# A hybrid encoder block on one core: the end rewritten, weight splits ordered behind bank readers, two kinds of operands loaded earlier, spilled tiles fetched among the kept

## The chip, the cores and the metric

The kernel runs on one core of a Trainium2 chip. The time is device microseconds of one execution; three runs of the kernel before gave a median of 917.51 us (916.77 to 918.26). The profile is of a further execution, which took 916.25 us. TensorE does the matrix products, VectorE and ScalarE the work on elements, GpSimd (POOL) and SyncE (SP) here mostly issue DMA transfers. Every engine runs its instructions in a fixed order.

## The reference

Two request groups ("prompt" and "sample", 1024 positions by 1024 channels each) go through one layer with shared weights:

```
h = rmsnorm(x, g_pre);  z = h @ w_in                      # 1024 -> 6 x 512
ya = pool_mixer(a_val) * silu(a_gate)                     # window means of 2/4/8/16, 128x128 maps
yb = short_conv(b_u, b_B, b_C) * silu(b_gate)             # width 3
o = concat(ya, yb) @ w_out;  x = x + rmsnorm(o, g_post)
gate = sigmoid(x @ w_ple_gate);  e = (p @ w_ple) * gate
y = x + rmsnorm(e, g_ple)
```

All is fp32. rmsnorm multiplies by 1/sqrt(mean(v*v) + 1e-6) over the 1024 channels and by a gain for each channel.

## The kernel before, in words

Activations lie with channels on the 128 partitions and positions along the free axis; a tile is 128 channels by 1024 positions, or a half of it, 512. An fp32 product is made of three matmuls on rounded parts: each operand is split into a high and a low part (`split`: a cast on ScalarE, L153, and a subtraction on VectorE, L154), and `mm` issues high*high, high*low and low*high at L293 to L295. Weights come from DRAM as raw blocks (`wraw`, three buffers), are split into halves (`whl`, eight buffers) and kept five halves ahead of TensorE (`AHEAD`). A scheduler orders the instructions of most of the program by their priorities; DMA issues and some additions are pinned to program order, and at the start and in the end the order on TensorE, ScalarE and VectorE is written out.

The work comes in stages. Stage A is the input projection of group 0, then of group 1: twelve pairs of weight blocks each. Stage B is the output projection, four pairs each. But for the first pair, a pair is done with seven products in place of eight (`pair_seven`, on sums and differences of operands; weights are summed at L210). A product has 12 matmuls of 128x512. Its seven kinds of operands (`KINDS`: n11, n21, z, t1, t3, t4, n22) are written to DRAM ahead of time, and when a group or a stage ends, 28 of them (4 of each kind) are loaded (`load_unit`) through six small buffers (`s`) and split. `take_place` does that for one kind, as soon as the last pair has used the old one; before the first of them `drain` empties the queue of background steps. A product goes to a bank of PSUM; ScalarE copies three of the results out (L507, L515, L522), and the next product into the same bank waits for that copy, as the bank `y` is used for four products.

The post-norm of group 0 (`norm_b`) runs as background steps inside stage B of group 1: sums of squares are added over the channels by matmuls with a matrix of ones, the root is made with logarithm, exponential and one Newton step (`rstd_l`), and for each of eight tiles VectorE multiplies by gain and root (L728) and GpSimd adds the product to the residual x1 in DRAM (L127). Three of the eight tiles are spilled to DRAM (`od`, `SPILL`), fetched again after the five kept ones are done (L124).

Last comes the gate: pieces of 24 matmuls, for each a sigmoid on ScalarE (L828), a multiply by the other factor (`pled`, loaded from DRAM by SP) on VectorE (L829), a square (L354) and an addition to the sum of squares (L355). The last four pieces of the last half of group 1 are done in two parts of 256 positions each (`finish`), so that the norm and the results of the first part lie beside the matmuls of the second. The results are y = e * r (L935), plus x1 (L937), and stores.

Of the kernel before, what the change touches and what calls it, by code (L numbers as in the profile page):

```python
# [16 lines left out]
P = 128  # L17
# [26 lines left out]

AHEAD = 5
# [4 lines left out]
TAIL = 4  # L50
FILL = 2, 2, 3
# [3 lines left out]
def tile_hybrid_encoder(ctx: ExitStack, tc, x, p, par, w_in, w_pool, w_out, w_gate, w_ple, y):  # L55
# [38 lines left out]
    nc.vector.memset(eps, EPS)  # L94
    one = const.tile([P, P], F32, name="one")
    nc.vector.memset(one, 1.0)
    nc.vector.tensor_copy(out=ones, in_=one)
    nc.scalar.mul(gneg, par_sb[:, G_PRE : G_PRE + KD], -1.0)
# [38 lines left out]

    def col(i):
        return par_sb[:, i : i + 1]
# [11 lines left out]

    def split(hi, lo, src):
        nc.scalar.copy(out=hi, in_=src)  # L153
        nc.vector.tensor_tensor(out=lo, in0=src, in1=hi.bitcast(F32), op=ALU.subtract)  # L154
# [24 lines left out]
    def hl_tile():  # L179
        return wpool.tile([P, 2, H, P], F32R, name="whl", tag="whl", bufs=HLBUFS)  # L180

    def split_half(src):
        hl = hl_tile()
        split(hl[:, 0], hl[:, 1], src)
        return hl
# [114 lines left out]
    def rstd_steps(acc, tmp, out=None, wait=1):  # L300

        n = acc.shape[1]
        u = unit()
        split(u[:, 0, :n], u[:, 1, :n], acc)
        for _ in range(wait):
            yield
        ps = psn.tile([P, C], F32, name="psn")[:, :n]  # L310
        nc.tensor.matmul(ps, ones, u[:, 0, :n], start=True, stop=False)
        nc.tensor.matmul(ps, ones, u[:, 1, :n], start=False, stop=True)
        r, v = (t[:, :n] for t in pair())
        a = tmp
        tc.keep_in_program_order(nc.scalar.preload_act_table_set("natural_log_exp_and_others"))
        nc.scalar.activation(out=r, in_=ps, func=AF.Ln, bias=eps, scale=1.0 / D)
        nc.scalar.activation(out=v, in_=ps, func=AF.Identity, bias=eps, scale=1.0 / D)
        nc.scalar.activation(out=r, in_=r, func=AF.Exp, scale=-0.5)
        yield
        nc.vector.tensor_tensor(out=a, in0=r, in1=v, op=ALU.mult)  # L320
        nc.vector.scalar_tensor_tensor(out=a, in0=a, scalar=-0.5, in1=r, op0=ALU.mult, op1=ALU.mult)
        out = r if out is None else out
        nc.vector.scalar_tensor_tensor(out=out, in0=a, scalar=1.5, in1=r, op0=ALU.add, op1=ALU.mult)
        yield
        return out

    def rstd_l(acc, out, wait=1):
# [6 lines left out]
        v, a = T()[:, :L], T()[:, :L]  # L334
        ps = [psn.tile([P, C], F32, name="psn") for c in range(NCH)]
        for p, u in zip(ps, us):
            nc.tensor.matmul(p, ones, u[:, 0], start=True, stop=False)
            nc.tensor.matmul(p, ones, u[:, 1], start=False, stop=True)
        tc.keep_in_program_order(nc.scalar.preload_act_table_set("natural_log_exp_and_others"))
# [5 lines left out]
        nc.vector.tensor_tensor(out=a, in0=out, in1=v, op=ALU.mult)  # L345
        nc.vector.scalar_tensor_tensor(out=a, in0=a, scalar=-0.5, in1=out, op0=ALU.mult, op1=ALU.mult)
        nc.vector.scalar_tensor_tensor(out=out, in0=a, scalar=1.5, in1=out, op0=ALU.add, op1=ALU.mult)
# [129 lines left out]
    def product(ps, units, first):  # L477
        mm(ps, [next_half()], operand(units), range(H), first, True, not first)
        product_done()

    def emit(dst, ps, add=None, neg=False):

        if add is None:
            nc.scalar.mul(dst, ps, -1.0 if neg else 1.0)
        elif neg:
            nc.vector.scalar_tensor_tensor(out=dst, in0=ps, scalar=-1.0, in1=add, op0=ALU.mult, op1=ALU.subtract)  # L486
        else:
            nc.vector.tensor_tensor(out=dst, in0=ps, in1=add, op=ALU.add)
# [13 lines left out]
    def pair_seven(h, use):  # L502
# [4 lines left out]
        nc.scalar.copy(out=p, in_=y)  # L507
# [7 lines left out]
        nc.scalar.copy(out=u, in_=y)  # L515
# [6 lines left out]
        nc.scalar.copy(out=g, in_=y)  # L522
# [195 lines left out]
    def norm_b(s, acc, kept):  # L718
# [7 lines left out]
        def add(k):  # L726
            pinned(
                nc.vector.scalar_tensor_tensor(  # L728
                    out=got[k], in0=got[k], scalar=col(G_POST + k), in1=r, op0=ALU.mult, op1=ALU.mult
# [26 lines left out]


# [41 lines left out]
    class Gate:  # L799
# [19 lines left out]
        def piece(self, d, c, w, i=0, n=C):  # L819

            o = i * n
            if i == 0 and d % 2 == 0:
                self.fetch()
            e = self.e(c, d)[:, o : o + n]
            z = bank()[:, :n]
            mm(z, w, operand(x1u[self.s][c], o, n), range(KD))
# [22 lines left out]
        def norm(self, c):  # L849

            s = self.s
            r = yield from rstd_steps(self.accs[c], small(), None, 4)
# [9 lines left out]
            for j in range(KD // 2):  # L862
                for i in range(2):
                    e = self.e(c, 2 * j + i)
                    nc.vector.scalar_tensor_tensor(
                        out=e, in0=e, scalar=col(G_PLE + 2 * j + i), in1=r, op0=ALU.mult, op1=ALU.mult
# [7 lines left out]
        def finish(self):  # L874
# [4 lines left out]
            s, c, n = self.s, NCH - 1, C // 2  # L879
# [105 lines left out]
    def run(steps):  # L985
        for _ in steps:
            pass
# [283 lines left out]
```

## Time and profile before

| | |
|---|---|
| median of three runs | 917.51 us |
| profiled execution | 916.25 us, of which 914.4 us is the span from first to last instruction |
| TensorE busy | 876.5 us (96%), 3830 matmuls |
| VectorE busy | 721.9 us (79%) |
| ScalarE busy | 483.5 us (53%) |
| GpSimd busy | 124.4 us (14%) |
| mean granted TensorE clock | 0.990 of 2.4 GHz |

Busy time is the time in which an engine executes something; with TensorE at 96%, what matters is where its few idle microseconds lie, and what it waited for there. Matmuls overlap: a 128x512 matmul is shown with 0.39 us, but the next starts 0.23 us after it. "<-" names what ended a wait: "<-ACT s L522" means that ScalarE's instruction of line 522, writing a tile named s, let it go. PE is TensorE, ACT ScalarE, DVE VectorE, POOL GpSimd, SPq the DMA issues of SP.

### The profile page before, as it was taken

To read this page: it belongs to the slowest core of one execution; us is meant where nothing else is said; L and a number is where in the kernel's file an instruction comes from. 1 tells how busy PE (TensorE), PEld (TensorE's weight loads), DVE (VectorE), ACT (ScalarE), POOL (GpSimd) and SP (SyncE) were. 2 spreads that over 40 slices of the span, in tenths; PEclk is the share of its full clock that TensorE was granted. 3 is DMA by queue.
4 is the path that set the end of the run, shared out by engine and by line. 5 is a ranking of instruction groups with operands and counts; after the bars stand their busy time and mean duration, and the time that the engine had idled before them with its cause. 6 is when DMAs were issued, how large, how long until landed. Compare 5 with 4: busy or idle time off the path is not lost.

```text
span 914.4 us, 11123 instructions
## 1 busy us (share of the span) xinstructions
PE 876.5 (96%) x3830; PEld 706.3 (77%) x3830; DVE 721.9 (79%) x1090; ACT 483.5 (53%) x829; POOL 124.4 (14%) x222
## 2 busy tenths in 40 slices
PE   6999999999999999999999999999998999999992
PEld 4787887888888788888888877887776788888892
DVE  5799999988668998586776988868878675678566
ACT  6967754333335743333333377447735653666743
POOL 0111111330000023201011100100021012013230
PEclk9999999999999999999999999999999999999996
DMA  9751645662215776756244367437398649859994
GB/s 341 294 184 58 200 147 206 217 251 73 89 51 158 253 256 219 265 183 237 97 173 162 128 221 254 180 116 230 115 230 218 220 103 273 268 128 280 295 307 165
DMA packets 65721, 179.31 MB, mean 196 GB/s; under 512 B 7296, under 2 KB 10880, under 8 KB 65664
## 3 DMA queue, kind: packets, MB, share of 16 engines
q1 hardware_dynamic: 39504, 98.84, 31.9%
q0 software_dynamic: 26016, 79.70, 28.9%
q8 instruction: 30, 0.49, 0.2%
q14 instruction: 27, 0.22, 0.1%
q10 hardware_dynamic: 144, 0.05, 0.0%
HBM read 127.72 MB, written 65.54 MB: 211 GB/s over the span
## 4 chain that ended last, share of the span: by engine, by line
PE 80%; DMA 7%; DVE 6%; ACT 4%; issue 2%; SPq 0%; DVEq 0%; ACTq 0%
PE z L293 26%; PE z L295 26%; PE z L294 26%; DMA s<-ykept_t 2%; DMA t<-x_d 1%; ACT u L153 1%; DMA t<-od 1%; DVE u L154 1%; DMA s<-yd 1%; DMA t<-p_d 1%; DVE u L463 1%; DVE t L937 1%; DVE t L728 1%; DMA x1d<-t 1%; DMA s<-kept_z 0%
## 5 line engine op out<-in xcount | busy, mean ns | idle before, releaser
L293 PE MATMUL z<-u,whl 128*128 128x512 f32 (+1 forms) x1188 | 461.6, 390 | 11.4 <-ACT s L522 8.8
L295 PE MATMUL z<-u,whl 128*128 128x512 f32 (+1 forms) x1188 | 460.0, 389 | 0.5 <-DVE whl L154 0.5
L294 PE MATMUL z<-u,whl 128*128 128x512 f32 (+1 forms) x1188 | 460.2, 388 | 0.0
L293 PEld LDWEIGHTS z<-u,whl 128*128 128x128 f32 x1188 | 223.3, 188 | 67.0 <-ACT s L522 12.5
L295 PEld LDWEIGHTS z<-u,whl 128*128 128x128 f32 x1188 | 223.6, 188 | 50.6 <-DVE whl L154 0.9
L294 PEld LDWEIGHTS z<-u,whl 128*128 128x128 f32 x1188 | 223.4, 188 | 49.4
L153 ACT CAST whl<-wsum 128x512 fp32r<-128x512 f32 x124 | 75.7, 619 | 101.3 <-PE z L295 48.4
L153 ACT CAST whl<-wraw 128x512 fp32r<-128x512 f32 x145 | 88.4, 619 | 61.2 <-PE z L295 52.7
L154 DVE TENSOR_TENSOR whl<-wraw,whl 128x512 fp32r<-128x512 f32 x145 | 97.8, 685 | 18.3 <-ACT whl L153 18.1
L154 DVE TENSOR_TENSOR whl<-wsum,whl 128x512 fp32r<-128x512 f32 x124 | 84.0, 685 | 24.6 <-ACT whl L153 24.1
L154 DVE TENSOR_TENSOR u<-s,u 128x512 fp32r<-128x512 f32 x92 | 61.2, 688 | 23.7 <-ACT u L153 22.9
L153 ACT CAST u<-s 128x512 fp32r<-128x512 f32 x92 | 55.3, 619 | 28.0 <-DMA s<-x1d 14.8
L210 DVE TENSOR_TENSOR wsum<-wraw 128x512 f32<-128x512 f32 x62 | 42.6, 687 | 31.0 <-DMA wraw<-w_in_d 26.3
L127 POOL DMA_DIRECT2D x1d<-t x40 | 38.5, 1198 | 204.2 <-DVE t L728 135.4
L153 ACT CAST u<-t 128x512 fp32r<-128x512 f32 x71 | 41.3, 622 | 26.4 <-DVE t L570 9.3
L354 ACT ACTIVATE s<-t 128x512 f32<-128x512 f32 (+1 forms) x60 | 36.1, 603 | 32.4 <-DVE t L829 17.3
L154 DVE TENSOR_TENSOR u<-t,u 128x512 fp32r<-128x512 f32 x71 | 45.6, 685 | 8.8 <-ACT u L153 8.5
L355 DVE TENSOR_TENSOR t<-t,s 128x512 f32<-128x512 f32 (+1 forms) x60 | 39.0, 652 | 10.6 <-ACT s L354 9.5
L124 POOL DMA_DIRECT2D yd<-t x16 | 8.7, 546 | 251.7 <-DVE t L623 166.3
L515 ACT COPY s<-z 128x512 f32<-128x512 f32 x31 | 18.1, 584 | 37.7 <-PE z L295 33.4
L522 ACT COPY s<-z 128x512 f32<-128x512 f32 x31 | 18.1, 583 | 35.9 <-PE z L295 35.9
L486 DVE SCALAR_TENSOR_TENSOR t<-z,s 128x512 f32<-128x512 f32 x46 | 31.4, 684 | 5.7 <-PE z L295 5.7
(121 smaller groups left out, 798.5 us busy)
## 6 DMA issues: line engine op xcount, KB each, us to landing
wraw<-w_in_d SPq DMA_DIRECT2D x48, 512.0 KB, 3.8
wraw<-w_gate_d SPq DMA_DIRECT2D x24, 512.0 KB, 6.1
pled<-t POOLq DMA_DIRECT2D x16, 512.0 KB, 3.8
t<-x_d POOLq DMA_DIRECT2D x16, 512.0 KB, 5.4
yd<-t POOLq DMA_DIRECT2D x16, 512.0 KB, 3.3
t<-yd POOLq DMA_DIRECT2D x16, 512.0 KB, 5.7
x1d<-x_d POOLq DMA_DIRECT2D x8, 1024.0 KB, 11.8
wraw<-w_out_d SPq DMA_DIRECT2D x16, 512.0 KB, 3.7
```

What stands on the lines that cost most here:

```text
L127: pinned(nc.gpsimd.dma_start(out=out, in_=in_, accum_op=ALU.add))
L153: nc.scalar.copy(out=hi, in_=src)
L154: nc.vector.tensor_tensor(out=lo, in0=src, in1=hi.bitcast(F32), op=ALU.subtract)
L210: nc.vector.tensor_tensor(out=t, in0=a, in1=b, op=ALU.add)
L293: nc.tensor.matmul(ps, wk[:, 0, kw, :], hi, start=a, stop=False, skip_group_check=on)
L294: nc.tensor.matmul(ps, wk[:, 0, kw, :], lo, start=False, stop=False, skip_group_check=on)
L295: nc.tensor.matmul(ps, wk[:, 1, kw, :], hi, start=False, stop=z, skip_group_check=on)
L354: nc.scalar.activation(out=tmp, in_=src, func=AF.Square)
L355: nc.vector.tensor_tensor(out=acc, in0=acc, in1=tmp, op=ALU.add)
L486: nc.vector.scalar_tensor_tensor(out=dst, in0=ps, scalar=-1.0, in1=add, op0=ALU.mult, op1=ALU.subtract)
L515: nc.scalar.copy(out=u, in_=y)
L522: nc.scalar.copy(out=g, in_=y)
```

## The change

It has five parts. The names are those of the code; line numbers of the changed kernel are higher by 5 to some 50.

1. *The end* (`finish`). Five pieces in place of four are cut into two parts of 256 positions (`TAIL`, `PARTS`, `FILL`). The sum of squares of a part is taken in two steps into the same place in PSUM: that of the first seven pieces (`most`), and that of the last piece, whose square goes straight into the split (`square`). The root of the first part (`root`) stands amid the matmuls of the second part's first piece. The Newton step reads PSUM. Weights of the two halves beyond eight go into ordinary tiles (`spare`).
2. *Roots.* `rstd_steps` and `rstd_l` no longer make the mean with a pass of ScalarE (Identity); the Newton step reads the sum in PSUM, with the gains multiplied by sqrt(D) once at the start. It is done in halves of 512.
3. *Reader order.* The copies and sums that read a product's bank are noted (`reader`), and a weight split gets an order behind those of the product four back on its own engine, without a semaphore (`behind_readers`).
4. *Early operands.* At a change of group or stage, `after` calls `take_place` two product steps earlier (`EARLY`), so for two kinds in the pair before last, and `drain` with it.
5. *Spilled tiles.* `norm_b` fetches the three spilled tiles after the third, fourth and fifth kept tile's addition, no longer after all five.

```diff
-TAIL = 4
-FILL = 2, 2, 3
+EARLY = 2
+READERS = 5
+TAIL = 5
+PARTS = 256, 256
+FILL = 5, 2, 1, 1, 2
...
+    readers = deque([[]], maxlen=READERS)
...
+    def behind_readers(ins):
+        if len(readers) == READERS:
+            for q in readers[0]:
+                if q.ins.engine == ins.ins.engine:
+                    tc.add_manual_dep(
+                        ins.ins,
+                        q.ins.name,
+                        mybir.DependencyInfo(mybir.DependencyClass.NoSync, mybir.DependencyReason.DATA),
+                        reason="behind a product's readers",
+                    )
...
     def split_half(src):
-        hl = hl_tile()
-        split(hl[:, 0], hl[:, 1], src)
+        if spare:
+            spare.pop()
+            hl = tpool.tile([P, 2, H, P], F32R, name="u", tag="t")
+        else:
+            hl = wpool.tile([P, 2, H, P], F32R, name="whl", tag="whl", bufs=HLBUFS)
+        for ins in split(hl[:, 0], hl[:, 1], src):
+            behind_readers(ins)
         return hl
...
+    def guess(r, ps):
+        nc.scalar.activation(out=r, in_=ps, func=AF.Ln, bias=eps)
+        nc.scalar.activation(out=r, in_=r, func=AF.Exp, scale=-0.5)
+
+    def newton(r, ps, a):
+        nc.vector.scalar_tensor_tensor(out=a, in0=ps, scalar=D * EPS, in1=r, op0=ALU.add, op1=ALU.mult)
+        yield
+        nc.vector.scalar_tensor_tensor(out=a, in0=a, scalar=-0.5, in1=r, op0=ALU.mult, op1=ALU.mult)
+        yield
+        nc.vector.scalar_tensor_tensor(out=r, in0=a, scalar=1.5, in1=r, op0=ALU.add, op1=ALU.mult)
+        yield
...
-        for p, o, w in zip(ps, halves(out), halves(v)):
-            nc.scalar.activation(out=o, in_=p, func=AF.Ln, bias=eps, scale=1.0 / D)
-            nc.scalar.activation(out=w, in_=p, func=AF.Identity, bias=eps, scale=1.0 / D)
-        nc.scalar.activation(out=out, in_=out, func=AF.Exp, scale=-0.5)
+        for p, q in zip(ps, halves(r)):
+            guess(q, p)
+        yield
+        for p, q, a in zip(ps, halves(r), pair()):
+            run(newton(q, p, a))
...
-        for k in range(SPILL[s], KD):
+        spilt = deque(range(0 if s else SPILL[s]))
+        for i, k in enumerate(range(SPILL[s], KD)):
             add(k)
             yield
-            yield
-        for k in range(SPILL[s]):
-            if not s:
-                fetch(k)
-                yield
+            if spilt and i >= 2:
+                fetch(spilt.popleft())
+            yield
...
+                def most(part):
+                    hi, lo = part.us[0]
+                    nc.scalar.copy(out=hi, in_=part.acc)
+                    nc.vector.tensor_tensor(out=lo, in0=part.acc, in1=hi.bitcast(F32), op=ALU.subtract)
+
+                def square(part):
+                    e, (hi, lo) = self.e(c, KD - 1)[:, part.cs], part.us[1]
+                    nc.scalar.activation(out=hi, in_=e, func=AF.Square)
+                    nc.vector.tensor_tensor(out=part.q, in0=e, in1=e, op=ALU.mult)
+                    nc.vector.tensor_tensor(out=lo, in0=part.q, in1=hi.bitcast(F32), op=ALU.subtract)
...
+                for n in PARTS:
+                    part = Part(o, n)
+                    for i, (d, w) in enumerate(zip(last, ws)):
+                        amid = (lambda: root(before)) if before and not i else None
+                        piece = self.piece(d, c, w, o, n, amid)
+                        if d < KD - 1:
+                            run(piece)
+                        else:
+                            next(piece)
+                            total(part.ps, part.us[0], True, False)
+                        if before and not i:
+                            for q in last:
+                                scale(q, before.cs)
+                            steps = before.rest()
+                        if before and d < KD - 1:
+                            fill(FILL[i])
+                        if d == KD - 2:
+                            part.most()
+                    part.square()
+                    before, o = part, o + n
+                root(part)
...
     def after(stage, s, j, n):
         pump(AHEAD)
-        if j == (NPAIR if stage == "A" else KD // 2) - 1:
-            if n == 0:
-                drain()
-                product_done(LATER)
-            take_place(stage, s, n)
-        else:
+        early = 0 if stage == "B" and s else EARLY
+        to_last = (NPAIR if stage == "A" else KD // 2) - 1 - j
+        kind = n + early - to_last * len(KINDS)
+        if kind == 0:
+            drain()
+            product_done(LATER)
+        if 0 <= kind < len(KINDS):
+            take_place(stage, s, kind)
+        if kind < 0:
             tick(1)
```

Three places show how the order of instructions moves. First GpSimd in the post-norm of group 0; `x1d0_...` is the residual that the tiles are added to, `od0_0`, `od0_1` and `od0_2` the spilled tiles. Before:

```order
L127 DMA x1d0_2_122<-t_5118 256x1x512
L127 DMA x1d0_2_122<-t_5175 256x1x512
L127 DMA x1d0_3_123<-t_5262 256x1x512
L127 DMA x1d0_3_123<-t_5399 256x1x512
L124 DMA t_5852<-od0_0_117 128x1024
L124 DMA t_5877<-od0_1_118 128x1024
L124 DMA t_5879<-od0_2_119 128x1024
L127 DMA x1d0_0_120<-t_5852 256x1x512
L127 DMA x1d0_0_120<-t_5877 256x1x512
```

The changed kernel:

```order
L135 DMA x1d0_2_124<-t_5117 256x1x512
L135 DMA x1d0_2_124<-t_5174 256x1x512
L132 DMA t_5727<-od0_0_119 128x1024
L135 DMA x1d0_3_125<-t_5301 256x1x512
L132 DMA t_5764<-od0_1_120 128x1024
L135 DMA x1d0_3_125<-t_5438 256x1x512
L132 DMA t_5837<-od0_2_121 128x1024
L135 DMA x1d0_0_122<-t_5727 256x1x512
L135 DMA x1d0_0_122<-t_5764 256x1x512
```

The fetches have moved from behind the fifth addition to behind the third, fourth and fifth, so the fourth and fifth additions now stand behind fetches.

Second, ScalarE at the change from group 0 to group 1 in stage A; a cast `u<-s` splits a loaded operand, and the copy `s<-z` (L522, L568 after) empties the bank. Before:

```order
L153 CAST u_2608<-s_2607 128x512
L153 CAST whl_2794<-wraw_2548 128x512
L153 CAST u_2613<-s_2612 128x512
L153 CAST u_2618<-s_2617 128x512
L153 CAST u_2623<-s_2622 128x512
L153 CAST whl_2835<-wraw_2502 128x512
L153 CAST u_2655<-s_2654 128x512
L522 COPY s_2686<-z_2467 128x512
L153 CAST u_2660<-s_2659 128x512
```

The changed kernel:

```order
L185 CAST u_2647<-s_2646 128x512
L185 CAST u_2652<-s_2651 128x512
L185 CAST whl_2813<-wraw_2587 128x512
L185 CAST u_2657<-s_2656 128x512
L185 CAST u_2662<-s_2661 128x512
L185 CAST u_2694<-s_2693 128x512
L185 CAST u_2699<-s_2698 128x512
L568 COPY s_2725<-z_2466 128x512
L185 CAST u_2704<-s_2703 128x512
```

Before, the copy stands behind the first cast of the kind t1 (u_2655); after, two kinds more have been loaded, and it stands behind the second cast of t4 (u_2694, u_2699).

Third, VectorE in the end, first part: L829 (L880 after) multiplies a piece by its pled tile (t_7472 before, t_7440 after is the last pled tile loaded). Before:

```order
L829 TENSOR_TENSOR t_7380<-t_7380,s_7517 128x256
L355 TENSOR_TENSOR t_6907<-t_6907,s_7517 128x256
L829 TENSOR_TENSOR t_7380<-t_7380,s_7547 128x256
L355 TENSOR_TENSOR t_6907<-t_6907,s_7547 128x256
L829 TENSOR_TENSOR t_7472<-t_7472,s_7577 128x256
L355 TENSOR_TENSOR t_6907<-t_6907,s_7577 128x256
L829 TENSOR_TENSOR t_7472<-t_7472,s_7607 128x256
L355 TENSOR_TENSOR t_6907<-t_6907,s_7607 128x256
L908 CAST u_7480<-t_6907 128x256
L909 TENSOR_TENSOR u_7480<-t_6907,u_7480 128x256
```

The changed kernel:

```order
L880 TENSOR_TENSOR t_7280<-t_7280,s_7480 128x256
L396 TENSOR_TENSOR t_6907<-t_6907,s_7480 128x256
L880 TENSOR_TENSOR t_7378<-t_7378,s_7510 128x256
L396 TENSOR_TENSOR t_6907<-t_6907,s_7510 128x256
L880 TENSOR_TENSOR t_7378<-t_7378,s_7540 128x256
L396 TENSOR_TENSOR t_6907<-t_6907,s_7540 128x256
L880 TENSOR_TENSOR t_7440<-t_7440,s_7570 128x256
L396 TENSOR_TENSOR t_6907<-t_6907,s_7570 128x256
L963 TENSOR_TENSOR u_7453<-t_6907,u_7453 128x256
L880 TENSOR_TENSOR t_7440<-t_7440,s_7602 128x256
L969 TENSOR_TENSOR t_7452<-t_7440 128x256
```

Before, the first multiply with the last pled tile (d=6) belongs to the third half piece, and a whole piece (d=3) stands ahead of the three; now it belongs to the fourth half piece, and d=3 is a half as well. The subtraction for the ones sum (L963) now follows the addition of d=6, ahead of the last piece's multiply.

## Rows read from the trace of the kernel before

**Rows 1.** The page's busy times: us, share, instructions.

```profile
PE 876.5 (96%) x3830; PEld 706.3 (77%) x3830; DVE 721.9 (79%) x1090; ACT 483.5 (53%) x829; POOL 124.4 (14%) x222
```

**Rows 2.** TensorE by stretches: window, us, busy (matmuls), granted clock, DMA share, GB/s.

```profile
275.00:300.00 25.00, 25.00 (x110) 1.00 0.54 169
...
300.00:325.00 25.00, 23.31 (x100) 1.00 0.79 272
...
675.00:700.00 25.00, 22.19 (x89) 0.93 0.93 238
```

**Rows 3.** TensorE's waits, 300 to 725 us: total, times, longest.

```profile
PE z L293 <- ACT s L522: 8.8, 7, 2.8
```

**Rows 4.** Timeline at 301 us: start, duration, engine, line, out<-in, count, idle before.

```profile
302.97 0.58 ACT L522 COPY s<-z 128x512 f32<-128x512 f32 x1
...
303.60 0.50 PE L293 MATMUL z<-u,whl 128*128 128x512 f32 x1 [1.69 <-ACT s L522]
```

**Rows 5.** TensorE's waits, 540 to 570 us.

```profile
PE z L293 <- ACT s L522: 1.9, 2, 1.1
...
PE z L293 <- ACT s L515: 0.4, 1, 0.4
```

**Rows 6.** TensorE's waits, 620 to 650 us.

```profile
PE z L293 <- ACT s L522: 1.0, 1, 1.0
...
PE z L293 <- ACT u L153: 0.9, 1, 0.9
```

**Rows 7.** TensorE's waits, 660 to 672 us.

```profile
PE z L293 <- ACT s L515: 0.9, 1, 0.9
...
PE z L293 <- ACT s L522: 0.7, 1, 0.7
...
PE z L293 <- DVE t L486: 0.3, 1, 0.3
```

**Rows 8.** Timeline near 690 us, VectorE, ScalarE and TensorE.

```profile
683.99 1.28 DVE L728 SCALAR_TENSOR_TENSOR t<-t,par_sb 128x1024 f32<-128x1024 f32 x1 [5.05 <-DMA t<-od]
...
690.08 0.58 ACT L522 COPY s<-z 128x512 f32<-128x512 f32 x1
...
690.71 0.50 PE L293 MATMUL z<-u,whl 128*128 128x512 f32 x1 [2.81 <-ACT s L522]
...
692.25 0.63 PE L295 MATMUL z<-u,whl 128*128 128x512 f32 x1
...
692.67 0.63 PE L293 MATMUL z<-u,whl 128*128 128x512 f32 x1
```

**Rows 9.** The chain that ended last: start, duration, engine, what.

```profile
668.69 4.80 DMA x1d<-t
...
673.49 10.40 DMA t<-od
```

**Rows 10.** Timeline of the program's end, from the last gate matmul.

```profile
896.01 0.28 PE L295 MATMUL z<-u,whl 128*128 128x256 f32 x1
...
901.17 0.58 PE L912 MATMUL psn<-u,ones 128*128 128x256 f32 x1 [4.88 <-DVE u L908]
...
905.80 0.69 DVE L935 TENSOR_TENSOR t<-t 128x512 f32<-128x512 f32 x1
...
910.51 0.69 DVE L937 TENSOR_TENSOR t<-t 128x512 f32<-128x512 f32 x1
```

**Rows 11.** Timeline of the end's first part, and a pass of ScalarE before it.

```profile
860.96 0.69 ACT L317 ACTIVATE t<-psn,eps 128x512 f32<-128x512 f32 x1
...
866.71 0.49 SPq L119 DMA_DIRECT2D t<-pled  x1
...
882.10 0.39 ACT L828 ACTIVATE s<-z 128x256 f32<-128x256 f32 x1 [1.49 <-PE z L295]
...
883.75 0.43 DVE L829 TENSOR_TENSOR t<-t,s 128x256 f32<-128x256 f32 x1 [2.69 <-DMA t<-pled]
...
884.89 0.39 ACT L828 ACTIVATE s<-z 128x256 f32<-128x256 f32 x1 [0.26 <-PE z L295]
```

More of the change, by code (lines that the diff above doesn't have):

```diff
@@ L136, in product_done, with run @@
             load(*late.popleft()[1:])
+    def run(steps):
+        for _ in steps:
+            pass
     def col(i):
@@ L298, in operand, with tables, total, rstd_steps @@
         return lambda k: (units[k][:, 0, o : o + n], units[k][:, 1, o : o + n])
-    def rstd_steps(acc, tmp, out=None, wait=1):
-        n = acc.shape[1]
+    def guess(r, ps):
[8 more added lines that the diff above has]
+        yield
+    def tables():
+        return nc.scalar.preload_act_table_set("natural_log_exp_and_others")
+    def total(ps, u, first=True, last=True):
+        nc.tensor.matmul(ps, ones, u[0], start=first, stop=False)
+        nc.tensor.matmul(ps, ones, u[1], start=False, stop=last)
+    def rstd_steps(acc, tmp, r, wait=1):
         u = unit()
-        split(u[:, 0, :n], u[:, 1, :n], acc)
+        split_unit(u, acc)
         for _ in range(wait):
             yield
[L310 to L318, printed above, removed]
+        ps = psn.tile([P, C], F32, name="psn")
+        total(ps, (u[:, 0], u[:, 1]))
+        pinned(tables())
+        guess(r, ps)
         yield
[L320 to L323, printed above, removed]
+        run(newton(r, ps, tmp))
         yield
-        return out
-    def rstd_l(acc, out, wait=1):
+    def rstd_l(acc, r, wait=1):
         us = [unit() for c in range(NCH)]
@@ L506, in pair_seven @@
         p = small()
-        nc.scalar.copy(out=p, in_=y)
+        reader(nc.scalar.copy(out=p, in_=y))
         yield
@@ L514, in pair_seven @@
         u = small()
-        nc.scalar.copy(out=u, in_=y)
+        reader(nc.scalar.copy(out=u, in_=y))
         yield
@@ L521, in pair_seven @@
         g = small()
-        nc.scalar.copy(out=g, in_=y)
+        reader(nc.scalar.copy(out=g, in_=y))
         use(1, 1, v, g)
@@ L947, in finish @@
                 for d in range(KD - TAIL):
-                    gain(d)
-                for d, w in zip(last, ws):
-                    run(self.piece(d, c, w, 0, n))
-                h[0].split()
-                run(self.piece(last[0], c, ws[0], 1, n))
-                h[0].sums()
-                tables()
-                h[0].guess()
-                for d in last:
-                    gain(d, 0)
-                h[0].newton()
-                first = h[0].results()
+                    scale(d)
@@ L961, in fill @@
+                before, steps = None, iter(())
                 def fill(k):
                     for _ in range(k):
-                        next(first, None)
-                fill(1)
-                for i in range(1, TAIL - 1):
-                    run(self.piece(last[i], c, ws[i], 1, n))
-                    fill(FILL[i - 1])
-                final = self.piece(last[-1], c, ws[-1], 1, n)
-                next(final)
-                fill(1)
-                run(final)
-                tables()
@@ L977, in finish @@
+                root(part)
                 for d in last:
-                    gain(d, 1)
+                    scale(d, part.cs)
                 fill(FILL[-1])
-                h[1].newton()
-                second = h[1].results()
-                run(first)
-                run(second)
-    def run(steps):
-        for _ in steps:
-            pass
+                last_steps = part.rest()
+                for k in range(3):
+                    next(last_steps)
+                run(steps)
```

126 lines of the change are left out of this document (61 added, 65 removed).

## The prediction, made before the changed kernel ran

> **What bounds the kernel now.** I read the page's busy times first, then the waits of TensorE, then the stretches in which matmuls are missing, then the timeline there. TensorE is busy for 876.5 us, 96% of the span [rows 1]: it is the bound, and only time in which it stands still, or runs at a lower clock, can be won by moving work. In a stretch without waits 25 us hold 110 matmuls, 0.227 us each; a product is 12 of them, 2.73 us [rows 2]. At the two changes of request group, at the change from stage A to B and in the post-norm of the first group the count falls to 100, and to 89 in one stretch [rows 2]. From 300 to 725 us the ScalarE copy at L522 alone keeps TensorE waiting 8.8 us in 7 waits [rows 3]. That copy (the eviction of the third product of a pair) is short, but ScalarE runs in order, and ahead of it stand casts whose load has not landed: at 301.5 us the product was done, the copy began at 302.97, TensorE went on at 303.60 after 1.69 us [rows 4]. The same pattern costs 1.9 + 0.4 us between 540 and 570 [rows 5], 1.0 + 0.9 us between 620 and 650 [rows 6], and 0.9 + 0.7 + 0.3 us between 660 and 672 [rows 7]. What is left of the 8.8 is 2.8 us at 690.71 and 0.7 us near 709.
>
> The wait at 690.71 has a chain of its own [rows 8, 9]: GpSimd issues the fetch of the first spilled tile at 673.49, behind the add of the last kept tile, and it takes 10.40 us to land; VectorE, in order, stands 5.05 us before the multiply at L728 that reads it; behind that come the weight sums, behind these ScalarE's splits, behind these the copy L522 at 690.08. After the 2.81 us TensorE runs eight matmuls at 0.43 us each, as from 692.25 to 692.67, and the stretch's granted clock is 0.93 [rows 2, 8]; that is 8 x (0.43 - 0.23) = 1.6 us more. So this place costs 4.4 us, and all waits of the interior with it 1.7 + 2.3 + 1.9 + 1.9 + 4.4 + 0.7 = 12.9 us.
>
> At the end, TensorE's last gate matmul starts at 896.01 and ends by 896.3; the last add on VectorE starts at 910.51 and ends at 911.2 [rows 10]: 14.9 us of a chain through ScalarE, VectorE, a cold TensorE (4.88 us idle before the sum) and eight multiplies and adds of 0.7 us.
>
> **The change, part by part.** *Spilled tiles.* The fetches now stand behind the third, fourth and fifth add on GpSimd. The third add was issued before the one at 668.69 whose landing took 4.80 us [rows 9], so the first fetch can go at about 668 and land by 668 + 10.4 = 678.4 even with the worst time seen. VectorE comes free for it only at 683.99 - 5.05 = 678.94 [rows 8], so its stall goes at either end. The second and third are read 2.4 and 6.3 us behind it by the old timeline, and their fetches stand 5 and 8 us earlier than before. The order on ScalarE also has the copy before the splits now. What is late next is the weight sums on VectorE, which go on without a pause. Bounds: 0 to 4.4 us won; I take 4.0.
>
> *Early operands.* The 28 loads of a change still pass six small buffers, but begin two products, 5.5 us, earlier. At 301 us the late load was late by less than that. Against a full gain stands the order: the copy L522 (L568 after) is now behind casts of the kind after the next one, that is, behind more casts, not fewer; SP's weight loads queue behind the loads that wait for a small buffer, but five weight halves, 13.7 us, stand ready as cover. The emptying of the background queue comes two products earlier as well. Of 1.7, 2.3 and 1.9 us I take 1.1, 1.2 and 1.0, somewhat over half. Bounds: the whole 5.9 won; or lost, at the price of the worst row (2.8 + 1.6 us) at each of the three places, 13.2 us. Because evictions and casts now mix in an order that no trace shows, I charge one new wait of the mean size, 8.8 / 7 = 1.3 us.
>
> *Square roots.* The Identity pass disappears; it delays the next instruction on ScalarE by about 0.6 us (0.69 us long [rows 11]), twice in the post-norm and once in every gate norm, and VectorE's pass is split in halves. In the post-norm this and the earlier fetch give 1.0 of the 1.9 us (bounds 0 and 1.9); at the program's start two such passes stand before the first operands: 0.3 us (bounds 0 and 1.2). Elsewhere TensorE has its products ready and nothing is won.
>
> *Reader order.* A weight split now never overtakes a reader of the product four back on its own engine. No instruction is added. The cover is the five halves ahead of TensorE, 13.7 us, against a reader that is at most a few us late; nothing. If that cover went, TensorE would wait for a weight; the bound is again 4.4 us a time.
>
> *The end.* Five half-width pieces in place of four: one whole piece becomes two halves, which costs TensorE nothing but the four more sums of ones, some 0.6 us with the reload of weights. Behind its last matmul the chain shrinks: the square goes straight into the split, the accumulated sum is already in PSUM, the copy of the variance is gone and the roots read PSUM. With VectorE's durations [rows 10] I count sigmoid 0.45, multiply, square and subtract 3 x 0.45, two cold sums 1.05, logarithm and exponential 0.95, three steps 1.4, eight results 5.4, and 0.8 for ten handovers: 11.4 us against 14.9. Less the 0.6 that is 2.9 us won, if nothing is late. But something is. The piece d=6 needs the last load of the gate's other factor (pled), which SP issues at 866.71 behind four loads of the residual, and VectorE's multiply waits for it until 883.75 [rows 11]; the sigmoid that it also needs was done at 882.10 + 0.39, so pled is 1.3 us late. The issue order on SP is unchanged in the changed kernel, and what releases it comes only 0.6 us earlier (the Identity pass ahead of the split on ScalarE). The first half of d=6, however, comes 2.7 us sooner, as one piece before it is now a half (a half takes 2.79 us, from the sigmoid at 882.10 to that at 884.89). So pled will be 1.3 + 2.7 - 0.6 = 3.4 us late. This time TensorE waits too: behind the first halves stands a sum of ones that needs the square of d=6, where the old program had a further half piece to do. Its wait: pled at 883.7 - 0.6, plus multiply, square, add, cast and subtract, 2.0 us, against the end of its half pieces at 882.2 (884.89 less 2.7): 883.1 + 2.0 - 882.2 = 2.9 us; the cast may start on what is ready and the load may gain from lighter traffic, so 2.3 to 3.3, and I take 2.5. That eats the 2.9.
>
> The trace shows TensorE at half clock for eight matmuls after a wait of 2.81 us [rows 8] and at full clock, 1.00 over the stretch, after 1.69 us [rows 2, 4]. 2.5 us is nearer to the former; by its row the price is 1.6 us, and I take 1.4 since the pieces are of half width: the end then loses 1.0 us in all; without it, it wins 0.4. The Trainium skill (TensorE: Matmul & The Clock Gate, "HAM oscillation") says that idle stretches of TensorE send it back to half rate and that it returns slow; it speaks against this part of the change, and the trace at 690.71 agrees with its 0.43 us matmuls; by the rule the end stands at a loss of 1.0 us, without it at a gain of 0.4.
>
> **Sum.** 4.0 + 1.1 + 1.2 + 1.0 + 1.0 + 0.3 - 1.3 - 1.0 = 6.3 us. The profiled execution took 916.25 us (914.4 and 1.85 around it), so 909.95; the median of the runs is 1.26 above it, so 911.2 us.
>
> **Rivals.** (A) As above, 909 to 914: 0.50. (B) The pled load lands in time, because the stretch before it moves less data or begins earlier: no wait, no slow clock; 911.2 - 2.5 - 1.4 = 907.3, with a full interior gain 905. For it: the transfer's length is all queueing (its issue took 17 us to land); against: the same loads stand ahead of it. 0.17. (C) Early loads only move the waits: the 3.3 us of the transitions are not won, 914.5; for it: six small buffers and more casts ahead of the copy. 0.16. (D) Slower: in the pair before last the evictions' own small tiles come from the same six buffers as the eight early loads; an eviction then has to wait until a load has landed and been cast, TensorE stops, and as at 690.71 comes back slow. At 4.4 us for each of three changes: 917.5 - 4.0 - 1.0 - 0.3 + 1.0 + 13.2 = 926; it decides from the point where the new waits pass 7.6 us in all, say 920. For it: the loads are what made evictions late; against: they start when ScalarE has few evictions behind. 0.11. (E) The change doesn't shorten what it means to: split order and longer queues take back what the fetches give, 917: 0.06.
>
> **Numbers.** Likeliest 911.2; A and B and most of C lie between 905.5 and 917, which leaves out D and some of B's end. A measurement of this kernel tells 0.2%, 1.8 us, from no change. Faster than 915.7: A, B, nearly all of C: 0.82; slower than 919.3: D, 0.11; between: E and a little of C, 0.07.
>
> **What would show it.** Right: the fetch issued near 668 (less what was won before) and no idle VectorE before its multiply; no 0.43 us matmuls near 690; the waits for the copy (L568 in the changed kernel) about 4 us in all; a TensorE wait of 2 to 3 us at the sum of ones behind the first halves, with slow matmuls behind it, and 11 to 12 us from the last gate matmul to the last add. Wrong: VectorE not waiting for pled (B), waits at 295 to 305 and 540 to 565 as long as before (C), evictions waiting for loads in the pair before last (D).

## The result, and the profile after

The changed kernel takes 925.12 us (median of eight runs, lowest 920.13) against 917.88 us before; the ratio is 1.0066 (95% interval 1.0047 to 1.0085). One of the eight runs took 2246.04 us, for a reason that the record does not show; the ratio leaves it out and is not that of the medians. The changed kernel is slower by 0.7%, where 911.2 us and a chance of 0.11 for slower were forecast. The profiled execution took 920.62 us, a span of 918.9 us; it is one of the shorter runs, and what the others lose beyond it no profile shows.

The page's busy times of the changed kernel (us, share of the span, instructions), and TensorE in stretches (window, us, busy with the number of matmuls, granted clock, DMA share, GB/s), the changed kernel's first, then one of the kernel before:

```profile
PE 879.8 (96%) x3858; PEld 711.6 (77%) x3858; DVE 721.4 (79%) x1099; ACT 478.7 (52%) x827; POOL 124.2 (14%) x222
```

```profile
300.00:325.00 25.00, 23.17 (x94) 0.93 0.72 249
375.00:400.00 25.00, 20.75 (x83) 0.93 0.88 308
625.00:650.00 25.00, 22.05 (x88) 0.93 0.74 234
650.00:675.00 25.00, 25.00 (x110) 1.00 0.48 99
675.00:700.00 25.00, 23.64 (x103) 1.00 1.06 243
875.00:900.00 25.00, 20.74 (x164) 0.93 0.97 270
```

```profile
375.00:400.00 25.00, 25.00 (x110) 1.00 0.87 304
```

TensorE is no less busy than before, but in other places. 675 to 700 us got better (103 for 89 [rows 2]), 300 to 325 worse (94 for 100 [rows 2]). A new hole stands at 375 to 400 us (83 matmuls), a stretch that before held 110 at clock 1.00 and that the prediction did not look at. If for every matmul the time from its start to the next start, beyond the usual pitch (0.227 us, at half width 0.116), is added up from the two timelines, without what is under 0.09 us, the places compare so:

| place, us | lost before | lost after |
|---|---|---|
| start, 0 to 100 | 7.0 | 5.7 |
| group 0 to 1 in stage A, 275 to 325 | 2.2 | 4.5 |
| 375 to 400 | 0 | 6.1 |
| stage A to B, 525 to 600 | 3.3 | 3.2 |
| group 0 to 1 in stage B, 600 to 650 | 2.9 | 5.0 |
| post-norm of group 0, 650 to 700 | 7.6 | 1.6 |
| both sums of ones in the end, 875 on | 5.4 | 7.9 |

**The new hole.** VectorE between 379 and 389 us (start, duration, engine, line, what, count, idle time before and what ended it), first in the kernel before, then in the changed one:

```profile
379.53 0.68 DVE L488 TENSOR_TENSOR t<-z,s 128x512 f32<-128x512 f32 x1
380.13 0.68 DVE L154 TENSOR_TENSOR whl<-wraw,whl 128x512 fp32r<-128x512 f32 x1
387.69 0.69 DVE L210 TENSOR_TENSOR wsum<-wraw 128x512 f32<-128x512 f32 x1 [6.88 <-DMA wraw<-w_in_d]
```

```profile
379.69 0.69 DVE L186 TENSOR_TENSOR whl<-wsum,whl 128x512 fp32r<-128x512 f32 x1
387.99 0.69 DVE L247 TENSOR_TENSOR wsum<-wraw 128x512 f32<-128x512 f32 x1 [7.62 <-DMA wraw<-w_in_d]
388.60 0.68 DVE L534 TENSOR_TENSOR t<-z,s 128x512 f32<-128x512 f32 x1
```

And TensorE after:

```profile
384.70 0.40 PE L332 MATMUL z<-u,whl 128*128 128x512 f32 x1
389.34 0.50 PE L330 MATMUL z<-u,whl 128*128 128x512 f32 x1 [4.25 <-DVE t L534]
...
390.56 0.63 PE L331 MATMUL z<-u,whl 128*128 128x512 f32 x1
390.99 0.63 PE L332 MATMUL z<-u,whl 128*128 128x512 f32 x1
```

In both programs VectorE stands some 7 us at a weight sum until a raw block lands (8 us after its issue; the median of these loads is 3.7 us). Before, the reader of a bank (L488) had run ahead of it, and the wait cost nothing. After, the two have changed places in VectorE's order, 80 us behind the loads that were moved. TensorE waits 4.25 us for the bank, and comes back with eight matmuls at 0.43 us, the pitch of the lower clock (the stretch's granted clock is 0.93).

**The end.** SP, VectorE and TensorE in the changed kernel:

```profile
869.40 0.38 SPq L127 DMA_DIRECT2D t<-pled  x1
```

```profile
886.99 0.42 DVE L880 TENSOR_TENSOR t<-t,s 128x256 f32<-128x256 f32 x1 [5.30 <-DMA t<-pled]
...
888.81 0.58 PE L356 MATMUL psn<-u,ones 128*128 128x256 f32 x1 [4.26 <-ACT u L962]
...
890.08 0.41 PE L332 MATMUL z<-u,whl 128*128 128x256 f32 x1
890.29 0.41 PE L330 MATMUL z<-u,whl 128*128 128x256 f32 x1
...
904.84 0.28 PE L332 MATMUL z<-u 128*128 128x256 f32 x1
...
914.95 0.69 DVE L981 TENSOR_TENSOR t<-t 128x512 f32<-128x512 f32 x1
```

This is the wait that was forecast [rows 11], only longer: 4.26 us, and half-width matmuls at 0.21 in place of 0.12 us behind it. From the last gate matmul's end at 905.1 to the last add's at 915.6 it is 10.5 us, where before it was 14.9 [rows 10]. Counted from the first gate matmul of group 1's last half to the last instruction, the end takes 65.72 us, where before it took 63.66.

**The post-norm.** VectorE no longer waits for a spilled tile, but TensorE has a new wait:

```profile
677.52 0.69 DVE L534 TENSOR_TENSOR t<-z,s 128x512 f32<-128x512 f32 x1 [2.26 <-DMA x1d<-t]
...
678.27 0.50 PE L330 MATMUL z<-u,whl 128*128 128x512 f32 x1 [1.36 <-DVE t L534]
```

The reader L534 writes its result into a tile that GpSimd's addition to the residual still reads. The fetches take tiles of the same pool earlier, so the next result gets one that is not free yet. That it is the fetch which took the free tile is read from the program; the trace shows the wait for the addition (2.26 us on VectorE, 1.36 on TensorE).

### The profile page after: what moved, and what is told of

Same layout as the page of the kernel before. It is cut to its first block, busy times and chain, and to the rows that moved or that the text cites. A ratio compares the mean times of both kernels' runs of the same rounds, so it can differ in the third digit from the quotient of the medians.

```text
span 918.9 us, 11217 instructions
## 1 busy us (share of the span) xinstructions
PE 879.8 (96%) x3858; PEld 711.6 (77%) x3858; DVE 721.4 (79%) x1099; ACT 478.7 (52%) x827; POOL 124.2 (14%) x222
## 4 chain that ended last, share of the span: by engine, by line
PE 71%; DVE 11%; DMA 10%; ACT 5%; issue 3%; SPq 0%; DVEq 0%; ACTq 0%; POOLq 0%
PE z L330 24%; PE z L332 24%; PE z L331 23%; DMA t<-pled 2%; DVE u L186 2%; DMA wraw<-w_in_d 2%; DVE whl L186 1%; DMA s<-ykept_t 1%; ACT u L185 1%; DMA s<-yd 1%; DMA s<-kept_t 1%; DMA t<-yd 1%; DVE t L1070 1%; DMA x1d<-t 1%; DVE wsum L247 1%
## 5 line engine op out<-in xcount | busy, mean ns | idle before, releaser
L396 DVE TENSOR_TENSOR t<-t,s 128x512 f32<-128x512 f32 (+1 forms) x59 | 38.3, 652 | 11.2 <-ACT s L395 10.4
L568 ACT COPY s<-z 128x512 f32<-128x512 f32 x31 | 18.2, 586 | 47.4 <-PE z L332 47.2
L880 DVE TENSOR_TENSOR t<-t,s 128x512 f32<-128x512 f32 (+1 forms) x37 | 22.8, 615 | 20.8 <-ACT s L879 14.2
```

What stands on the lines that cost most here:

```text
L396: nc.vector.tensor_tensor(out=acc, in0=acc, in1=tmp, op=ALU.add)
L568: reader(nc.scalar.copy(out=g, in_=y))
L880: nc.vector.tensor_tensor(out=e, in0=e, in1=g, op=ALU.mult)
```

## The experiments

Ratios are to the kernel before, run on the same chip between them.

| kernel | median us | ratio (95%) |
|---|---|---|
| changed kernel | 925.1 | 1.0066 (1.0047 to 1.0085) |
| changed, late loads | 916.7 | 0.9993 (0.9973 to 1.0013) |
| changed, pled first | 918.2 | 1.0011 (0.9988 to 1.0034) |
| changed, one sum behind readers | 916.3 | 0.9986 (0.9966 to 1.0006) |
| changed, late loads, pled first | 912.3 | 0.9945 (0.9928 to 0.9961) |
| changed, one sum behind readers, pled first | 912.2 | 0.9939 (0.9917 to 0.9960) |
| before, early loads alone | 923.1 | 1.0056 (1.0036 to 1.0076) |
| before, spilled tiles among the kept alone | 918.3 | 1.0009 (0.9994 to 1.0024) |
| before, pled first alone | 916.5 | 0.9997 (0.9983 to 1.0011) |
| late loads, pled first, no split order | 912.3 | 0.9938 (0.9917 to 0.9958) |
| late loads, pled first, old fetch of spilled tiles | 911.4 | 0.9931 (0.9909 to 0.9953) |
| late loads, pled first, four pieces at the end | 913.3 | 0.9966 (0.9945 to 0.9986) |
| new end and roots only, pled first | 909.9 | 0.9935 (0.9912 to 0.9958) |

**Late loads** (of the changed kernel):

```diff
-EARLY = 2
+EARLY = 0
```

> The changed kernel with the operands of the next group loaded as late as before (EARLY = 0), all else as changed. Theory (the early loads do the harm: they move a weight sum ahead of a bank reader on VectorE, and bring evictions behind casts whose loads have not landed): the wait of 4.2 us near 389 us and the slow matmuls behind it are gone (6.1 us), the change of group in stage A loses 2.2 us again and not 4.5, the one in stage B 2.9 and not 5.0; in all 8 to 11 us less than the changed kernel, 910 to 915 us, faster than before by 3 to 7 us. Rival (the order of splits behind readers does the harm): the wait near 389 us stays, the time stays at 919 to 926 us.

0.9993 against 1.0066: 6.7 us better, somewhat less than expected. The hole near 389 us is gone:

```profile
300.00:325.00 25.00, 22.30 (x90) 0.93 0.76 246
375.00:400.00 25.00, 25.00 (x109) 1.00 0.84 298
```

The rival falls: the split order was still in. But the change of group in stage A does not get better with late loads (90 matmuls here, 94 with early ones). So the part of the theory that blamed the early loads alone for that place was wrong. By the timelines every variant with the new roots and end loses 4.1 to 5.9 us there, with early loads or late ones; the kernel before and its variants with late loads lose 2.2 to 2.4. But the kernel before with early loads (below) loses 4.5 us there too, so either is enough. What in the new roots and end does it was not separated, and stays open. For the change in stage B the theory held: 1.3 us are lost from 600 to 650 us, where the changed kernel loses 5.0.

**One sum behind the readers.** Early loads stay; one weight sum is given an order on VectorE behind the readers recorded before it:

```diff
+HELD_SUM = 65
...
-            nc.vector.tensor_tensor(out=t, in0=a, in1=b, op=ALU.add)
+            ins = nc.vector.tensor_tensor(out=t, in0=a, in1=b, op=ALU.add)
+            sums.append(ins)
+            if len(sums) == HELD_SUM:
+                for q in [q for q in chain(*readers) if q.ins.engine == ins.ins.engine][-6:][:1]:
+                    if q.ins.engine == ins.ins.engine:
+                        tc.add_manual_dep(
...
```

> The changed kernel with one weight sum (the one whose raw block lands at 388 us) ordered behind the readers recorded before it on VectorE; TensorE's, GpSimd's and SP's orders are unchanged. Theory (the wait at 389 us comes from that sum standing ahead of the reader in VectorE's order): the wait of 4.2 us and the eight slow matmuls go, 5 to 6.5 us less than the changed kernel, 914 to 920 us. Rival (the load itself is what TensorE waits for, as the next weights come from it): the wait only moves to a weight, less than 2 us won.

0.9986: 7.3 us better than the changed kernel by the ratios, a little more than was expected and than the 6.1 us of the hole. TensorE in that stretch:

```profile
375.00:400.00 25.00, 25.00 (x110) 1.00 0.88 319
```

Some 25 rows of VectorE's order moved with it, so it is not a pure swap, but the orders of TensorE, GpSimd and SP are those of the changed kernel. No weight came too late in its place.

**Early loads alone, in the kernel before:**

```diff
+EARLY = 2
...
-        if j == (NPAIR if stage == "A" else KD // 2) - 1:
...
+        early = 0 if stage == "B" and s else EARLY
+        to_last = (NPAIR if stage == "A" else KD // 2) - 1 - j
+        kind = n + early - to_last * len(KINDS)
...
```

> The kernel before with the early loads alone (EARLY = 2), all else as before. VectorE's order now has the same weight sum ahead of the same bank reader as in the changed kernel. Theory (the early loads alone make the wait near 389 us): that wait of 4 to 5 us with slow matmuls behind it appears, and the change of group in stage A loses more than before; 5 to 9 us slower than before, 922 to 926 us. Rival (the harm needs the other parts, the order of splits above all): within 2 us of before.

1.0056, as expected: 5.1 us slower. VectorE's order has the same swap, and the trace the same wait. VectorE, and TensorE's wait between 380 and 395 us:

```profile
391.07 0.69 DVE L212 TENSOR_TENSOR wsum<-wraw 128x512 f32<-128x512 f32 x1 [7.63 <-DMA wraw<-w_in_d]
391.68 0.68 DVE L490 TENSOR_TENSOR t<-z,s 128x512 f32<-128x512 f32 x1
```

```profile
PE z L295 <- DVE t L490: 4.3, 1, 4.3
```

So the early loads are enough to make the kernel slower, without the split order and without the new end; the rival falls.

**Pled first.** The last pled load goes ahead of the four residual loads on SP:

```diff
+            while self.fetches:
+                self.fetch()
             x1 = [T()[:, :L] for j in range(KD // 2)]
...
             pump(2 * TAIL)
-            while self.fetches:
-                self.fetch()
```

> The changed kernel with the last pled tile loaded ahead of the four residual tiles, all else as changed. Theory (TensorE's wait at the first sum of ones is the late pled tile): the tile lands by 878 us, the wait of 4.3 us near 884 us and the slow matmuls behind it go, 5 to 6 us less than the changed kernel, 915 to 920 us. Rival (the chain of square, addition and split behind d=6 is what TensorE waits for, whenever the tile lands): less than 1.5 us won.

1.0011: 5.0 us better than the changed kernel by the ratios. TensorE's waits from 870 us on, in this kernel:

```profile
PE psn L356 <- ACT u L962: 0.6, 1, 0.6
PE psn L356 <- ACT u L968: 0.4, 1, 0.4
```

The wait of 4.26 us is gone; what is left of 0.6 and 0.4 us is the chain of square and split, the rival's share, at the second part's end. Counted as above, the end takes 60.4 us, 5.3 less than in the changed kernel and 3.3 less than before.

In the kernel before, the same edit alone:

```diff
+            while self.fetches:
+                self.fetch()
             x1 = [T()[:, :L] for j in range(KD // 2)]
...
-            while self.fetches:
-                self.fetch()
```

> The kernel before with the last pled tile loaded ahead of the four residual tiles, all else as before. Theory (the old end has a further half piece for TensorE while VectorE waits for that tile, so the tile's lateness costs it nothing): within 1 us of before, though the wait of 2.7 us on VectorE near 884 us goes. Rival (the late tile already set the old end's time): 2 us or more faster.

0.9997: nothing. The old end didn't feel that the tile was late, as TensorE had a further half piece to do. The new end does.

**Both together**, late loads and pled first:

```diff
-EARLY = 2
+EARLY = 0
...
+            while self.fetches:
+                self.fetch()
             x1 = [T()[:, :L] for j in range(KD // 2)]
...
-            while self.fetches:
-                self.fetch()
```

> The changed kernel with both EARLY = 0 and the last pled tile ahead of the residual tiles. Theory: the two gains add, 905 to 910 us. Rival (waits that go make others longer, since the same loads then collide): 912 us or more.

0.9945: 4.5 to 5 us faster than before; the two gains (0.73% and 0.55%) add up to what is seen, 1.21%. The time expected was 2 us too low, and 912.3 us is by its number the rival's; against the rival stands that the two gains add.

Then the held-back sum and pled first, with early loads kept:

```diff
...
+                for q in [q for q in chain(*readers) if q.ins.engine == ins.ins.engine][-6:][:1]:
...
+            while self.fetches:
+                self.fetch()
             x1 = [T()[:, :L] for j in range(KD // 2)]
...
-            while self.fetches:
-                self.fetch()
```

> The changed kernel with early loads kept, the one weight sum behind the readers, and the last pled tile first. Theory (those two waits were all that the change lost by early loads and end together; the changes of group lose as much as with late loads): 910 to 913 us, equal within 2 us to the kernel with late loads. Rival (early loads are good where they don't move the sum): 908 us or less.

0.9939, the same as with late loads. The rival falls: where early loads don't move the sum, they win nothing that can be measured. The traces, one for each kernel, suggest that this hides a loss and a win. From 600 to 650 us, at the change of group in stage B, the five kernels with early loads lose 3.5 to 5.1 us and the nine with late ones 1.3 to 3.0; from 650 to 725 us, in the post-norm, it is 2.3 to 5.8 against 5.4 to 10.5.

**Without the split order**, beside late loads and pled first:

```diff
-READERS = 5
+READERS = 10**6
```

> EARLY = 0, the last pled tile first, and the splits' order behind readers taken out as well (READERS never reached). Theory (that order is worth nothing, as the weights are five halves ahead): within 1.5 us of the same kernel with it, 911 to 914 us. Rival (the order keeps evictions from standing behind splits): 3 us or more slower than with it, 915 us or more.

0.9938 against 0.9945 with it: nothing, as forecast.

**Spilled tiles.** First the changed kernel with late loads and pled first, and the old fetch:

```diff
-        spilt = deque(range(0 if s else SPILL[s]))
-        for i, k in enumerate(range(SPILL[s], KD)):
+        for k in range(SPILL[s], KD):
             add(k)
             yield
-            if spilt and i >= 2:
-                fetch(spilt.popleft())
             yield
+        for k in range(SPILL[s]):
+            if not s:
+                fetch(k)
+                yield
```

> EARLY = 0, the last pled tile first, and the spilled tiles fetched after all five kept tiles again, as before. Theory (the fetch among the kept is worth the 4.4 us near 690 us, less the new wait near 676 us of 2 to 3 us): 1 to 3 us slower than with the new fetch, 913 to 916 us, with the wait of 2.8 us near 690 us back. Rival (the new wait near 676 us eats all of it): equal within 0.7 us.

0.9931, no slower than with the new fetch (0.9945), where 1 to 3 us more were expected. Its trace has no wait near 690 us but one of 2.3 us near 707 us, so the expected return of the old wait is wrong as well. Then the new fetch alone, in the kernel before (the same lines the other way round):

> The kernel before with the spilled tiles fetched among the kept ones alone, all else as before. Theory (the wait of 2.8 us near 690 us goes, but a reader on VectorE then waits for a tile whose addition to the residual has not been made, as near 676 us in the changed kernel, and eats most of it): 0 to 2 us faster than before. Rival (my prediction's term: the wait and the slow matmuls behind it are worth 4.0 us): 3 to 4.5 us faster.

1.0009 (0.9994 to 1.0024): nothing won. The trace of it, VectorE, and TensorE's waits from 655 to 725 us:

```profile
675.54 0.69 DVE L488 TENSOR_TENSOR t<-z,s 128x512 f32<-128x512 f32 x1 [4.84 <-DMA x1d<-t]
```

```profile
PE z L293 <- DVE t L488: 3.9, 1, 3.9
PE z L293 <- ACT s L522: 1.4, 2, 0.7
```

The wait of 2.8 us near 690 is gone (before, L522 had 2.8 + 0.7 + 0.7 in this stretch), and one of 3.9 us for a tile of the pool stands 14 us earlier. The rival falls. The theory's 0 to 2 us held at its lower end alone: the new wait eats all of the old one, not most of it.

**The end with four pieces**, beside late loads and pled first:

```diff
-TAIL = 5
+TAIL = 4
-FILL = 5, 2, 1, 1, 2
+FILL = 5, 2, 2, 2
```

> EARLY = 0, the last pled tile first, and the new end with four pieces cut in halves in place of five (FILL 5, 2, 2, 2). Theory (what the new end wins is its shorter chain behind the last matmul, not the fifth piece): within 1 us of the same with five pieces, 911 to 913 us. Rival (the fifth piece is what gives the first part's results time): 2 us or more slower, 914 us or more.

0.9966 against 0.9945; the intervals overlap, the difference is 2 us. The traces bear it out: counted as above, the end takes 62.3 us with four pieces, and 60.3 to 60.6 in the six kernels with five pieces and pled first. So the fifth piece is worth 1.6 to 2.0 us here, and the theory was wrong.

**New end and roots only**, with pled first (the old fetch of the spilled tiles as above):

```diff
-EARLY = 2
+EARLY = 0
-READERS = 5
+READERS = 10**6
...
+            while self.fetches:
+                self.fetch()
             x1 = [T()[:, :L] for j in range(KD // 2)]
...
-            while self.fetches:
-                self.fetch()
```

> The changed kernel with EARLY = 0, no order of splits behind readers, the spilled tiles fetched after the kept as before, and the last pled tile first: only the new end and the new roots are left of the change. Theory (these two carry all that the change can win): 910 to 913 us, 5 to 7 us faster than before. Rival (the parts taken out add something once the pled tile is in time): 915 us or more.

0.9935 (0.9912 to 0.9958), 909.9 us: as fast as the fastest others. It holds two of the change's five parts and one load moved. It beats both kernels, and the three parts left out add nothing that these runs can tell. Of the 6.0 us, the end is 3.3 by the traces.

## Why the prediction was wrong, point by point

*Early operands* (forecast 3.3 us won, less 1.3 for a new wait): the step that failed. The forecast weighed the loads at the three changes of group and stage alone; it charged 1.3 us for a new wait and took 4.4 us for the worst that one could cost there. The worst came true and more (6.1 us, as the wait was longer), but in another place: the scheduler's order changed 80 us later, in a stretch without a wait before, where VectorE's idle 7 us at a weight sum had been harmless only because a reader stood ahead of it. The prediction never read that stretch. Early loads alone cost 0.56%; holding that sum back, with the loads kept early, gives back 0.8%.

The 3.3 us at the changes themselves did not come either; 3.6 us were lost there. What the prediction held against its gain, and rival C, shows in the changed kernel's ScalarE: the copy L568 stands behind casts whose loads have not landed, and TensorE's wait of 1.83 us at 307.48 ends with it.

```profile
304.02 1.72 ACT L185 CAST u<-s 128x512 fp32r<-128x512 f32 x3 [2.36 <-DMA s<-kept_t]
306.32 0.62 ACT L185 CAST u<-s 128x512 fp32r<-128x512 f32 x1 [0.58 <-DMA s<-kept_t]
306.85 0.58 ACT L568 COPY s<-z 128x512 f32<-128x512 f32 x1
```

How much of the 3.6 us is the early loads' and how much that of the new roots and end stays open, as said above.

*Spilled tiles* (forecast 4.0 us): failed too. The mechanism at 690 us was read rightly [rows 8, 9], and the fetch did come early (671.46 in the changed kernel, where 668 was forecast, and no idle VectorE before the multiply). What was left out is that a fetch takes a tile of the pool when it is issued; the next result of a product then waits for a tile whose addition has not ended. By itself the edit won nothing. From 650 to 700 us the changed kernel did lose 6.0 us less than before, more than the forecast for the spilled tiles and the post-norm's waits; but by their traces the new fetch alone loses more there (9.5 us) than the kernel before (7.6), and the early loads alone, with the old fetch, less (3.1). So that the number for this stretch came out was luck.

*The end* (forecast 1.0 us lost): right in mechanism and in sign, too small. The wait at the sum was 4.26 us and not 2.5, as SP issued the load at 869.40, 15.2 us ahead of the end of TensorE's half pieces (884.6), where 16.1 were reckoned, and it took 17.5 us where 17.0 were. The slow matmuls cost about 1.0 us (ten at 0.21) where 1.4 was taken. The shorter chain won 4.4 us against 3.5 forecast. All in all the end lost 2.1 us (65.72 for 63.66). With pled first the wait goes, and 5 us with it: rival B's mechanism, which needed one load moved. The end then wins 3.3 us; the prediction had reckoned 2.9 if nothing is late.

*Roots* at the start (forecast 0.3): 1.3 us less lost by the two timelines, of which 0.6 us are three fewer matmuls at 0.43 us in TensorE's first stretch, not shown to come from the roots. The wait for a split operand at 34 us is 0.65 us where it was 1.08 (first before, then after):

```profile
34.76 0.50 PE L293 MATMUL z<-u 128*128 128x512 f32 x1 [1.08 <-ACT u L153]
```

```profile
33.87 0.51 PE L330 MATMUL z<-u 128*128 128x512 f32 x1 [0.65 <-ACT u L185]
```

*Reader order* (forecast 0): right.

*Sum.* Forecast -6.3 us, profiled +4.4 us, 10.7 us apart. Up to the last half of the gate both programs have 3538 matmuls, so the start of the same matmul can be compared in the two timelines:

| matmul | start after, us | behind the kernel before, us |
|---|---|---|
| 1200 | 290.92 | -1.13 |
| 1500 | 364.84 | 1.07 |
| 2000 | 486.42 | 6.71 |
| 2500 | 605.23 | 6.22 |
| 2750 | 668.19 | 8.07 |
| 3000 | 728.60 | 2.14 |
| first of the last half of the gate | 853.14 | 2.38 |
| end of the span | 918.85 | 4.43 |

So the start won 1.1 us (0.3 forecast), the three changes lost 3.6 (3.3 to be won, less the 1.3), the hole lost 5.6 (nothing forecast), the post-norm won 5.9 (5.0 forecast), and the end lost 2.1 (1.0 forecast). The first table, which adds up single waits, has 4.3 for the changes and 6.1 for the hole; the two counts agree to 0.7 us. The single runs give much the same, each with some 2 us on either side: early loads alone lost 5.1 us, spilled tiles alone 0.8, the new end and roots won 1.0 (6.0 with pled first, less the 5.0 that pled first is worth in the changed kernel), the split order 0; that is 4.9 us of the 6.1 us of the ratio.

Of rival D the sign and the size came true, not its mechanism: the three copies that empty a bank waited 0.2 us in all for a small buffer, and for the rest for their product.

## What to carry to other kernels

Where a scheduler sets the order, compare the orders of the engines over the whole program, not only around the edit, and look in the trace of before for an in-order engine's long idle time that costs nothing: whatever stands just ahead of it is one swap away from waiting for it. A fetch brought forward takes its buffer earlier too, so ask who gets the next buffer of that pool. And when a stage is cut finer, move its loads with it: one load, issued four places earlier, was worth more here than the three scheduling edits together.

## What the runs showed that was not expected

With a wait of about 2 us, its length alone does not tell whether TensorE comes back slow. After 1.83 us at 307.48 in the changed kernel it ran eight matmuls at 0.43 us:

```profile
307.48 0.50 PE L330 MATMUL z<-u,whl 128*128 128x512 f32 x1 [1.83 <-ACT s L568]
...
309.18 0.63 PE L332 MATMUL z<-u,whl 128*128 128x512 f32 x1
309.61 0.63 PE L330 MATMUL z<-u,whl 128*128 128x512 f32 x1
```

After 1.69 us before the change it did not [rows 2, 4]. But in the kernel with one sum behind the readers it did not after 2.49 us either; the granted clock of that stretch is 1.00:

```profile
629.45 0.39 PE L343 MATMUL z<-u,whl 128*128 128x512 f32 x1
632.33 0.50 PE L342 MATMUL z<-u,whl 128*128 128x512 f32 x1 [2.49 <-ACT s L580]
```

```profile
625.00:650.00 25.00, 21.88 (x94) 1.00 0.51 166
```

So a wait of about 2 us may cost 1.6 us more or nothing, and what a new wait of that size costs is known only from its own trace. In all fourteen traces together, from 60 us up to the gate's half pieces, none of the 50 waits of TensorE of 1.0 to 1.75 us was followed by matmuls at 0.43 us, nine of the 19 waits of 1.8 to 2.7 us were, and all seven of 2.8 us and more.
